# A fifth summed chunk in the up-projection's couples, and the convolution's two older taps multiplied on ScalarE

## The chip, the cores and the metric

One NeuronCore of a Trainium2 chip runs the whole program in one launch; the other cores do nothing. The metric is the device time of one execution in microseconds (us), the median of several. The engines are TensorE (PE in the profile, its weight loads PEld), VectorE (DVE), ScalarE (ACT), GpSimd (POOL) and SyncE (SP), which run side by side and wait for each other through semaphores.

## The reference

A trunk of two layers over 256 positions and 2048 features, in float32. Layer 0 mixes tokens with a gated MLP, layer 1 with latent attention. Behind each mixer comes the part that is changed here, an MLP with a causal convolution of width 3 along the positions:

```python
def conv_ffn(x, w_up, conv_w, conv_b, w_down):
    h = x @ w_up                                  # 2048 -> 2 * 5504
    h = depthwise_causal_conv(h, conv_w) + conv_b # h[s]*w2 + h[s-1]*w1 + h[s-2]*w0 + b, per column
    a, g = jnp.split(h, 2, axis=-1)
    return (jax.nn.silu(g) * a) @ w_down          # 5504 -> 2048
```

Each sub-layer ends in x = LayerNorm(ALPHA * x + sublayer(x)).

## The kernel before, in words

**Three products for one.** Each float32 operand is split into a high part that TensorE takes (`hi`) and the rest (`lo`); a product is hi*hi + lo*hi + hi*lo. Activations come split as `xhl`. Weights are streamed: `Feed` (line 86) loads chunks of 1 MB into tiles `raw` (3 slots), ScalarE casts the high part `wh` (line 134), VectorE subtracts for the low part `wl` (line 137), and both go into tiles with the tag `big` (14 slots in all, shared with `xhl` and much else). `next` (line 210) hands out one chunk and puts the split of the chunks two further on into the program. The tag `side` has 6 slots, `t1` (tiles of 256 columns) 6, `t2` (512 columns) 5. A planner orders each engine's instructions when the program is built; on the chip each engine then works through its own list in order.

**Wide and summed chunks.** A wide chunk covers two blocks of 128 of the contraction, two halves of 128 positions and two pieces of 512 columns: eight products of 512 columns, three matmuls each, 24 in all (`eight`, line 439). A summed chunk (kind `seven`, line 140) gets the same with seven products, 21 matmuls, by Strassen's scheme in Winograd's form. For that VectorE first forms four sums of its weights (`ts`: one instruction of 1024 columns and two of 512, lines 148 to 151), and these are split as well (`th`, `tl`, line 153): two casts and two subtractions of 1536 columns and one each of 512. The activations need sums too; `combine` (line 319) makes them once for each chunk position, in rooms that hold two positions each.

**The up-projection.** For each layer the 86 column blocks of 128 (43 of the half `a`, 43 of the half `g`) are worked off in groups of two blocks of each half (group 21 has one). Most groups are plain (`plain`, line 1081): weights stand still, positions stream, 4 chunks, 128 matmuls, half of them of 512 columns and half of 256, into 4 of the 8 PSUM banks. Groups 5 with 6 and 8 with 9 are done as couples (`summed`, line 1106) with 8 chunks of the two kinds into all 8 banks. The order of a couple's chunks is `UP_PAIRS` = 0, 2, 1, 3, 5, 4, 6, 7, and `UP_SEVEN` names the summed ones. Around the plain groups 1 to 4 the table `EARLY` (line 76) hangs the making of the activations' sums and other small jobs behind given chunks. A couple's outputs have the positions in rows; in the next plain group they are turned back by TensorE and then go through the convolution there (`both`, line 1051).

**The convolution.** `conv` (line 1018) works on one column block, 128 partitions of 256 positions. From a plain group it first adds the two halves of a bank (`sum_halves`, line 407: ScalarE copies one half to `lo`, VectorE adds the other into `h`), which is what frees the bank; from a couple it reads the bank itself. ScalarE writes the newest tap with its bias into `c` (line 1023), and VectorE adds the two older taps with one fused multiply-add each (lines 1024 and 1026). `pair` (line 1034) does this for a block of `a` and of `g`, then ScalarE takes silu (line 1040) and VectorE multiplies (line 1041).

Of the kernel before, what the change touches and what calls it, by code (L numbers as in the profile page):

```python
# [8 lines left out]
F32 = mybir.dt.float32  # L9
F32R = mybir.dt.float32r  # L10
BF16 = mybir.dt.bfloat16
AF = mybir.ActivationFunctionType
ALU = mybir.AluOpType
AX = mybir.AxisListType

P = 128
S = 256
# [36 lines left out]

MO_SEVEN = (1, 2)

T1, T2 = 6, 5
SLOTS = {"big": 14, "raw": 3, "side": 6}


# [11 lines left out]

UP = [(1,), (2,), (3,), (4,), (5, 6), (7,), (8, 9), *((i,) for i in range(10, 22))]
UP_PAIRS = [0, 2, 1, 3, 5, 4, 6, 7]
UP_SEVEN = (2, 3, 4, 6)
EARLY = {(1, 2): ("restore", 0), (2, 1): ("combine", 0), (2, 2): ("restore", 1), (2, 3): ("park", 0),
         (3, 1): ("restore", 2), (3, 2): ("combine", 1), (3, 3): ("restore", 3), (4, 0): ("park", 1),
         (4, 1): ("combine", 2), (4, 2): ("combine", 3)}


def plan(n_k):
# [140 lines left out]
def trunk(ctx: ExitStack, tc: tile.TileContext, x, xT, gm_in, gm_wout, ffn_up, ffn_dn,  # L222
          ml_q, ml_kv, ml_b, ml_out, consts, w_sT, b_s, ropes, ln_rows, out):
    nc = tc.nc
# [3 lines left out]
    tp = ctx.enter_context(tc.tile_pool(name="tp", bufs=3))  # L228
# [6 lines left out]
    def slot(shape, name, dt=F32, tag="big"):  # L235
        return big.tile(shape, dt, tag=tag, name=name, bufs=SLOTS[tag])

    def bank(name):
        return ps.tile([P, 512], F32, tag="bank", name=name)
# [21 lines left out]
    for g in range(6):  # L261
        for p in U_PAIRS[g]:
            i = 48 + 8 * g + p // 2
            w = gm_in[i : i + 5 : 4, :, p % 2 * 1024 : p % 2 * 1024 + 1024].rearrange("f p c -> p f c")
# [14 lines left out]
    def up(w):  # L279

        for gis in ((0,), *UP):
# [3 lines left out]
            for p in UP_PAIRS:  # L285
                i = 4 * gis[0] + p // 2
                t = w[i : i + 5 : 4, :, p % 2 * 1024 : p % 2 * 1024 + 1024].rearrange("f p c -> p f c")
                chunks.append((t, 2048, "seven" if p in UP_SEVEN else "wide"))

# [29 lines left out]
    def combine(name, o, k1, k2):  # L319


        t = tp.tile([P, 4, P], F32, tag="t2", name=f"xs{name}", bufs=T2)
        turn(t, k1, k2)
        o = o.rearrange("p (h s c) -> p h s c", h=2, s=4)
        nc.scalar.copy(o[:, 0], t)
        nc.vector.tensor_tensor(o[:, 1], t, o[:, 0].bitcast(F32), ALU.subtract)
        return [(o[:, 0, i], o[:, 1, i]) for i in (1, 2, 0, 3)]
# [29 lines left out]
    cst = cpool.tile([P, N_CONST], F32, name="cst")  # L357
# [49 lines left out]
    def sum_halves(acc, name):  # L407
        lo = tp.tile([P, S], F32, tag="t1", name=f"lo_{name}", bufs=T1)
        nc.scalar.copy(lo, acc[:, S : 2 * S])
        h = tp.tile([P, S], F32, tag="t1", name=f"h_{name}", bufs=T1)  # L410
        nc.vector.tensor_tensor(h, acc[:, 0:S], lo, ALU.add)
        return h

    def split_act(src, name):

# [443 lines left out]
    for gi in range(6):  # L859

        acc = Banks(f"v{gi}", DIRECT if gi == 0 else OWN + DIRECT if gi % 2 else DIRECT + OWN)
# [99 lines left out]
    def turned(g, tiles):  # L961

        for i, t in enumerate(tiles):
            src = v[g][:, i // 2, i % 2 * 512 : i % 2 * 512 + 512]
            for j in range(4):
                nc.tensor.transpose(t[:, j * P : (j + 1) * P], src[:, j * P : (j + 1) * P], ident)
            nc.scalar.copy(src, t)
# [15 lines left out]
    for g in range(6):  # L983
        direct, own = (ub[4:], ub[:4]) if g % 2 else (ub[:4], ub[4:])
        acc = Banks(f"u{g}", DIRECT + OWN, direct + own)
# [29 lines left out]
    acc, end = down(NF_GM, pT, "wo", ln, acts, tiles=ub, beside=lambda: turned(5, ub[4:]))  # L1015


    def conv(layer, F, acc, name):

        h = acc if acc.shape[-1] == S else sum_halves(acc, name)  # L1020
        w = C_CONV + (layer * 2 * NF_FF + F) * 4
        c = tp.tile([P, S], F32, tag="t1", name=f"c_{name}", bufs=T1)
        nc.scalar.activation(c, h, AF.Identity, bias=cst[:, w + 3 : w + 4], scale=cst[:, w + 2 : w + 3])
        nc.vector.scalar_tensor_tensor(c[:, 1:S], h[:, 0 : S - 1], cst[:, w + 1 : w + 2], c[:, 1:S],
                                       ALU.mult, ALU.add)
        nc.vector.scalar_tensor_tensor(c[:, 2:S], h[:, 0 : S - 2], cst[:, w : w + 1], c[:, 2:S],
                                       ALU.mult, ALU.add)
        return c

    def ffn(layer, ln, acc, end, last):  # L1030
# [3 lines left out]
        def pair(a, acc_a, acc_g):  # L1034
            if act[a // 8] is None:
                act[a // 8] = slot([P, 8, S], f"act{layer}_{a // 8}", tag="side" if a // 8 in (0, 5) else "big")
            ca = conv(layer, a, acc_a, f"{layer}a{a}")
            cg = conv(layer, NF_FF + a, acc_g, f"{layer}g{a}")
            s = tp.tile([P, S], F32, tag="t1", name=f"s{layer}_{a}", bufs=T1)
            nc.scalar.activation(s, cg, AF.Silu)  # L1040
            nc.vector.tensor_tensor(act[a // 8][:, a % 8, :], s, ca, ALU.mult)
# [26 lines left out]
        sums, rooms = {}, []  # L1068

        def combine_up(p):  # L1070

            x = xhl[p // 2][:, p % 2 * 2 : p % 2 * 2 + 2]
            y = tp.tile([P, 2, S], F32, tag="t2", name=f"upy{layer}_{p}", bufs=T2)
            nc.vector.tensor_tensor(y, x[:, :, 0:S].bitcast(F32), x[:, :, S : 2 * S].bitcast(F32), ALU.add)
            if len(sums) % 2 == 0:
                rooms.append(slot([P, 2, 8 * P], f"xu{layer}_{p}", F32R))
            sums[p] = combine(f"u{layer}_{p}", rooms[-1][:, len(sums) % 2, :], y[:, 0], y[:, 1])

        early = {"restore": old.restore, "park": old.park, "combine": lambda i: combine_up(UP_SEVEN[i])}

        def plain(gi, turned):
# [24 lines left out]
        def summed(gis):  # L1106

            acc = Banks(f"up{layer}_{gis[0]}", DIRECT + OWN)
            for p in UP_PAIRS:
                a = [[x_parts(xhl, 2 * p + j, b) for j in range(2)] for b in range(2)]  # L1110
                got = feed.next()
                if p in UP_SEVEN:
                    acc.seven(a, sums[p], *got, turned=512, across=True)
                    if p == UP_SEVEN[-1]:
                        rest = acc.rest()
# [16 lines left out]
    ln, acc, end = ffn(0, ln, acc, end, False)  # L1132
# [61 lines left out]
    acc = [[bank(f"mkv{b}_{f}") for f in range(2)] for b in range(2)]  # L1194
    for c in range(6):
        hi, lo = feed.next()
# [34 lines left out]
    acc = [[bank(f"qr{b}_{f}") for f in range(2)] for b in range(2)]  # L1231
    for c in range(2):
        hi, lo = feed.next()
# [145 lines left out]
    for hf in range(2):  # L1379
        acc = [[bank(f"vv{hf}_{b}_{f}") for f in range(2)] for b in range(2)]  # L1380
        for c in range(2):
            hi, lo = feed.next()
# [10 lines left out]
        for b in range(2):  # L1393
            for f in range(2):
                c = slice(hf * 1024 + f * 512, hf * 1024 + (f + 1) * 512)
# [14 lines left out]
    acc = [[bank(f"mo0_{b}_{f}") for f in range(2)] for b in range(2)]  # L1410
    LAG = 4
    attend_c(0)
    for t in range(3, H + LAG):
        k = t - LAG
        if k >= 0:
            if k % 2 == 0:
                hi, lo = feed.next()
            w = slice((k % 2) * 1024, (k % 2) * 1024 + 1024)
# [19 lines left out]
    for c in range(8):  # L1438
        left = 7 - c
        got = feed.next(splits=2 if left > 5 else 3, loads=2)  # L1440
        if left < SKEW:
            for j in range(2):
                w = slice(j * 1024, (j + 1) * 1024)
# [10 lines left out]
    acc = [[second.acc[DIRECT[2 * b + f]] for f in range(2)] for b in range(2)]  # L1454
# [6 lines left out]
    ln, acc, end = ffn(1, ln, banks, end_mo, True)  # L1461
# [99 lines left out]
```

## Time and profile before

| | |
|---|---|
| time, median of 3 runs | 2450.97 us (2450.84 to 2450.98) |
| profiled execution | 2450.69 us, its span 2448.9 us |
| granted TensorE clock | full in all 40 slices of the page |
| matmuls | 12154 |
| DMA | 627.37 MB, mean 256 GB/s |

The span is the time from the first to the last instruction of the profiled execution; its own time is measured around it. Busy time of an engine counts the stretches in which at least one of its instructions is under way. Instructions on one engine overlap by a little, so a sum of durations is somewhat more than the time that they take back to back.

### The profile page before, as it was taken

What the parts mean: (1) busy time and instruction counts of PE and PEld (TensorE: products, weight loads), DVE (VectorE), ACT (ScalarE), POOL (GpSimd) and SP (SyncE); (2) the same over time, 40 slices, a digit from 0 to 9 for tenths busy, and PEclk for the clock granted to TensorE, in tenths of its full rate; (3) what the DMA queues carried; (4) which work ended last, traced back from release to release, by engine and by line L of the source; (5) the groups of instructions that cost most, each with busy time, mean ns of one, the idle gap of its engine ahead of it and who ended that gap; (6) DMA issues with size and microseconds to landing.
All of it is one profiled execution on the core that took longest, in us unless ns stands there. A gap on an engine that the chain in (4) does not pass through costs nothing.

```text
span 2448.9 us, 32246 instructions
## 1 busy us (share of the span) xinstructions
PE 2441.2 (100%) x12154; PEld 2066.0 (84%) x12154; DVE 2187.1 (89%) x2909; ACT 1510.8 (62%) x1995; POOL 140.2 (6%) x261
## 2 busy tenths in 40 slices
PE   9999999999999999999999999999999999999999
PEld 7888888888888888888888888988888888888887
DVE  7999999889998889998889897878798998888998
ACT  6666665566576655666665566665665666666553
POOL 0000000001010000011000000000000001010000
PEclk9999999999999999999999999999999999999999
DMA  7555666658796655799988885543575589898894
GB/s 293 204 206 206 232 202 206 206 172 302 256 296 241 239 203 194 260 356 377 338 322 320 317 299 170 189 143 126 205 275 180 179 337 363 321 368 304 313 353 178
DMA packets 128763, 627.37 MB, mean 256 GB/s; under 512 B 11592, under 2 KB 15184, under 8 KB 91616
## 3 DMA queue, kind: packets, MB, share of 16 engines
q1 hardware_dynamic: 94224, 462.47, 53.1%
q0 software_dynamic: 34384, 162.86, 17.8%
q8 instruction: 95, 1.56, 0.2%
q14 instruction: 60, 0.49, 0.1%
HBM read 552.35 MB, written 72.93 MB: 255 GB/s over the span
## 4 chain that ended last, share of the span: by engine, by line
PE 95%; DVE 2%; issue 1%; DMA 1%; ACT 1%; SPq 0%; ACTq 0%; DVEq 0%
PE up L242 29%; PE ub L242 16%; PE dn_q L242 8%; PE dn_p L242 6%; PE v_q L242 5%; PE v_p L242 4%; PE up_q L242 2%; PE wo_q L242 2%; PE dn_e L242 2%; PE up_p L242 2%; PE wo_p L242 2%; PE upf L242 2%; PE mo L242 2%; PE v_e L242 2%; PE mkv L242 1%
## 5 line engine op out<-in xcount | busy, mean ns | idle before, releaser
L137 DVE TENSOR_TENSOR wl<-raw,wh 128x1024 fp32r<-128x1024 f32 (+5 forms) x611 | 937.7, 1553 | 106.3 <-ACT wh L134 76.3
L134 ACT CAST wh<-raw 128x1024 fp32r<-128x1024 f32 (+5 forms) x611 | 791.2, 1318 | 312.9 <-PE up L242 72.0
L242 PE MATMUL up<-xhl,wh 128*128 128x512 f32 x2112 | 492.9, 390 | 0.0
L242 PEld LDWEIGHTS up<-xhl,wh 128*128 128x128 f32 x2112 | 392.3, 188 | 78.6
L134 ACT CAST th<-ts 128x1536 fp32r<-128x1536 f32 x194 | 201.5, 1052 | 164.2 <-DVE ts L144 136.9
L242 PEld LDWEIGHTS up<-xhl,wl 128*128 128x128 f32 x2112 | 262.4, 192 | 5.1
L242 PE MATMUL up<-xhl,wl 128*128 128x256 f32 x2112 | 265.1, 283 | 0.0
L137 DVE TENSOR_TENSOR tl<-ts,th 128x1536 fp32r<-128x1536 f32 x194 | 229.6, 1223 | 9.1 <-ACT th L134 4.7
L242 PE MATMUL ub<-wh,xhl 128*128 128x512 f32 x564 | 175.7, 393 | 0.0
L144 DVE TENSOR_TENSOR ts<-ts,raw 128x512 f32<-128x512 f32 x194 | 133.9, 690 | 2.0
L242 PEld LDWEIGHTS ub<-wh,xhl 128*128 128x128 f32 x564 | 105.9, 188 | 23.7 <-issue 1.9
L144 DVE TENSOR_TENSOR ts<-raw 128x1024 f32<-128x1024 f32 x97 | 118.5, 1222 | 2.7 <-DMA raw<-in_gm_in_dram 1.0
L242 PE MATMUL ub<-wl,xhl 128*128 128x512 f32 x282 | 109.8, 389 | 0.0
L242 PE MATMUL v_q<-wh,xhl 128*128 128x512 f32 x224 | 70.7, 391 | 0.1
L242 PEld LDWEIGHTS ub<-wl,xhl 128*128 128x128 f32 x282 | 53.0, 188 | 11.1
L242 PE MATMUL v_p<-wh,xhl 128*128 128x512 f32 x192 | 59.9, 389 | 0.0
L242 PEld LDWEIGHTS v_q<-wh,xhl 128*128 128x128 f32 x224 | 42.1, 188 | 9.7 <-ACT wh L134 1.0
L832 ACT ACTIVATE lny<-lnt,lncol 128x128 f32<-128x128 f32 x96 | 36.5, 469 | 15.7 <-PE lnt L828 15.6
L161 DVE TENSOR_TENSOR praw<-praw 128x512 f32<-128x512 f32 x64 | 44.1, 690 | 0.5
L242 PE MATMUL v_q<-wl,xhl 128*128 128x512 f32 x112 | 43.6, 389 | 0.0
L242 PE MATMUL mo<-wh,oT 128*128 128x512 f32 x128 | 42.7, 411 | 0.0
L242 PEld LDWEIGHTS v_p<-wh,xhl 128*128 128x128 f32 x192 | 36.1, 188 | 7.5
(2073 smaller groups left out, 4820.9 us busy)
## 6 DMA issues: line engine op xcount, KB each, us to landing
raw<-in_ffn_up_dram SPq DMA_DIRECT2D x172, 1024.0 KB, 5.7
raw<-in_gm_in_dram SPq DMA_DIRECT2D x93, 1024.0 KB, 5.2
raw<-in_ffn_dn_dram SPq DMA_DIRECT2D x68, 1024.0 KB, 7.9
raw<-in_gm_wout_dram SPq DMA_DIRECT2D x48, 1024.0 KB, 6.5
praw<-in_ffn_dn_dram POOLq DMA_DIRECT2D x16, 1024.0 KB, 12.8
keptth<-pth POOLq DMA_DIRECT2D x16, 1024.0 KB, 8.5
kepttl<-ptl POOLq DMA_DIRECT2D x16, 1024.0 KB, 8.8
fth<-keptth POOLq DMA_DIRECT2D x16, 1024.0 KB, 9.6
```

What stands on the lines that cost most here:

```text
L134: cast = self.nc.scalar.copy(hi, raw)
L137: self.nc.vector.tensor_tensor(lo, raw, hi.bitcast(F32), ALU.subtract)
L144: add = lambda o, a, b: self.nc.vector.tensor_tensor(o, a, b, ALU.add)
L161: add = lambda o, a, b: pin(nc.vector.tensor_tensor(o, a, b, ALU.add))
L242: recent[0] = nc.tensor.matmul(o, l, r, start=start, stop=stop, skip_group_check=True)
L832: nc.scalar.activation(y[:, j], t[:, j * P : (j + 1) * P], AF.Identity, bias=lncol[:, o : o + 1], scale=lncol[:, g : g + 1])
```

## The change

Chunk position 5 of every couple is summed as well, so a couple's chunks are wide, summed, wide, four summed, wide. Its activations' sums are made behind the last chunk of group 4. The rooms of the activations' sums (three now, two before) lie in `side` instead of `big`. The two older taps of the convolution are multiplied by ScalarE into a tile `d`, which VectorE adds to `c`; the first `d` reuses the tile `lo` where there is one, the other is a new tile, and `t1` has 7 slots instead of 6.

```diff
-T1, T2 = 6, 5
+T1, T2 = 7, 5
 SLOTS = {"big": 14, "raw": 3, "side": 6}
...
-UP_SEVEN = (2, 3, 4, 6)
+UP_SEVEN = (2, 3, 5, 4, 6)
 EARLY = {(1, 2): ("restore", 0), (2, 1): ("combine", 0), (2, 2): ("restore", 1), (2, 3): ("park", 0),
          (3, 1): ("restore", 2), (3, 2): ("combine", 1), (3, 3): ("restore", 3), (4, 0): ("park", 1),
-         (4, 1): ("combine", 2), (4, 2): ("combine", 3)}
+         (4, 1): ("combine", 2), (4, 2): ("combine", 3), (4, 3): ("combine", 4)}
...
         nc.vector.tensor_tensor(h, acc[:, 0:S], lo, ALU.add)
-        return h
+        return h, lo
...
-        h = acc if acc.shape[-1] == S else sum_halves(acc, name)
+        h, spare = (acc, None) if acc.shape[-1] == S else sum_halves(acc, name)
         w = C_CONV + (layer * 2 * NF_FF + F) * 4
         c = tp.tile([P, S], F32, tag="t1", name=f"c_{name}", bufs=T1)
         nc.scalar.activation(c, h, AF.Identity, bias=cst[:, w + 3 : w + 4], scale=cst[:, w + 2 : w + 3])
-        nc.vector.scalar_tensor_tensor(c[:, 1:S], h[:, 0 : S - 1], cst[:, w + 1 : w + 2], c[:, 1:S],
-                                       ALU.mult, ALU.add)
-        nc.vector.scalar_tensor_tensor(c[:, 2:S], h[:, 0 : S - 2], cst[:, w : w + 1], c[:, 2:S],
-                                       ALU.mult, ALU.add)
+        for j in range(2):
+            d = spare if spare is not None and j == 0 else tp.tile([P, S], F32, tag="t1", name=f"d{j}_{name}", bufs=T1)
+            nc.scalar.mul(d[:, 1 + j : S], h[:, 0 : S - 1 - j], cst[:, w + 1 - j : w + 2 - j])
+            nc.vector.tensor_tensor(c[:, 1 + j : S], c[:, 1 + j : S], d[:, 1 + j : S], ALU.add)
         return c
...
             if len(sums) % 2 == 0:
-                rooms.append(slot([P, 2, 8 * P], f"xu{layer}_{p}", F32R))
+                rooms.append(slot([P, 2, 8 * P], f"xu{layer}_{p}", F32R, "side"))
```

## Rows read from the trace of the kernel before

**Rows 1.** The page, part 1: busy time, share of the span, instructions of each engine.
```profile
PE 2441.2 (100%) x12154; PEld 2066.0 (84%) x12154; DVE 2187.1 (89%) x2909; ACT 1510.8 (62%) x1995; POOL 140.2 (6%) x261
```

**Rows 2.** The chain that ended last: shares; and a piece (start, us, what).
```profile
PE 95%; DVE 2%; issue 1%; DMA 1%; ACT 1%; SPq 0%; ACTq 0%; DVEq 0%
...
1467.23 5.44 PE dn_q L242 x24
```

**Rows 3.** Waits of TensorE and its weight loads: us in total, times, longest.
```profile
PE up_p L242 <- DVE h_1a L411: 0.5, 1, 0.5
...
PEld up_q L242 <- DVE tl L137: 0.8, 2, 0.4
```

**Rows 4.** Stretch, length; busy us PE, PEld, DVE, ACT, POOL; clock; DMA share, GB/s.
```profile
812.17:900.20 88.03, 88.03 (x511) 78.08 (x511) 77.14 (x127) 50.16 (x73) 1.81 (x3) 1.00 0.74 255
900.20:941.00 40.80, 40.80 (x181) 33.80 (x180) 37.04 (x42) 25.10 (x27) 0.00 (x0) 1.00 0.52 184
941.00:964.97 23.97, 23.97 (x145) 21.42 (x144) 22.41 (x36) 14.38 (x21) 0.00 (x0) 1.00 0.56 195
964.97:1006.17 41.20, 41.20 (x181) 33.62 (x180) 38.85 (x44) 24.48 (x27) 0.00 (x0) 1.00 0.54 189
1006.17:1263.68 257.51, 257.51 (x1490) 228.31 (x1489) 229.57 (x324) 166.61 (x231) 24.33 (x43) 1.00 0.91 345
...
1919.90:1961.80 41.90, 41.39 (x181) 33.59 (x180) 38.99 (x45) 25.09 (x29) 0.00 (x0) 1.00 0.55 188
```

**Rows 5.** Groups by line on VectorE: shapes, count, busy us, mean ns, idle before.
```profile
L137 DVE TENSOR_TENSOR wl<-raw,wh 128x2048 fp32r<-128x2048 f32 x146 | 333.4, 2292 | 57.9 <-ACT wh L134 51.7 <-PE dn_q L242 3.8
L137 DVE TENSOR_TENSOR tl<-ts,th 128x1536 fp32r<-128x1536 f32 x97 | 170.4, 1757 | 9.1 <-ACT th L134 4.7 <-PE v_p L242 1.9 <-PE ub L242 1.4
L137 DVE TENSOR_TENSOR wl<-raw,wh 128x1536 fp32r<-128x1536 f32 x97 | 170.3, 1755 | 3.8 <-PE v_q L242 2.5 <-PE up L242 0.8 <-PE mo L242 0.3
L144 DVE TENSOR_TENSOR ts<-ts,raw 128x512 f32<-128x512 f32 x194 | 133.9, 690 | 2.0
L144 DVE TENSOR_TENSOR ts<-raw 128x1024 f32<-128x1024 f32 x97 | 118.5, 1222 | 2.7 <-DMA raw<-in_gm_in_dram 1.0 <-PE ub L242 0.7 <-PE v_q L242 0.5
L137 DVE TENSOR_TENSOR tl<-ts,th 128x512 fp32r<-128x512 f32 x97 | 66.8, 689 | 0.0
L1041 DVE TENSOR_TENSOR act<-s,c_1a 128x256 f32<-128x256 f32 x43 | 18.2, 424 | 5.1 <-ACT s L1040 5.0
L1024 DVE SCALAR_TENSOR_TENSOR c_0g<-h_0g,cst,c_0g 128x255 f32<-128x255 f32 x33 | 15.9, 481 | 3.0 <-ACT c_0g L1023 3.0
```

**Rows 6.** VectorE in order of time, layer 0's couples: start, us, line, operation, [idle before].
```profile
906.33 2.29 DVE L137 TENSOR_TENSOR wl<-raw,wh 128x2048 fp32r<-128x2048 f32 x1 [1.31 <-ACT wh L134]
...
908.94 0.42 DVE L411 TENSOR_TENSOR h_0g<-up,lo_0g 128x256 f32<-128x256 f32 x1
...
930.51 2.35 DVE L137 TENSOR_TENSOR tl<-ts,th 128x1536 fp32r<-128x1536 f32 x2
...
983.23 2.29 DVE L137 TENSOR_TENSOR wl<-raw,wh 128x2048 fp32r<-128x2048 f32 x1
985.44 1.22 DVE L144 TENSOR_TENSOR ts<-raw 128x1024 f32<-128x1024 f32 x1
...
991.84 1.22 DVE L144 TENSOR_TENSOR ts<-raw 128x1024 f32<-128x1024 f32 x1
```

**Rows 7.** TensorE in order of time, at the first couple's chunk 6.
```profile
933.30 0.39 PE L242 MATMUL up_q<-tl,xhl 128*128 128x512 f32 x1
```

**Rows 8.** Groups by line on ScalarE: the convolution's present operations.
```profile
L1023 ACT ACTIVATE c_0g<-h_0g,cst 128x256 f32<-128x256 f32 x10 | 6.0, 602 | 7.6 <-DVE h_0g L411 7.6
L1040 ACT ACTIVATE s<-c_0g 128x256 f32<-128x256 f32 x43 | 17.9, 416 | 22.1 <-DVE c_0g L1026 22.1
L409 ACT COPY lo_0a<-up 128x256 f32<-128x256 f32 x33 | 11.9, 361 | 23.0 <-PE up L242 23.0
```

**Rows 9.** TensorE's weight loads in order of time, the first couple's second chunk.
```profile
909.50 0.41 PEld L242 LDWEIGHTS up_p<-th,xu 128*128 128x128 f32 x2
```

## The prediction, made before the changed kernel was run

> **What bounds the kernel now.** I read the engines' totals first: TensorE is busy for 2441.2 of 2448.9 us, VectorE for 89%, ScalarE for 62% [rows 1]. A busy TensorE need not be one at its peak, so the second view is the chain of work that ended last: 95% of it is TensorE, and its pieces give the rate, 24 matmuls of 512 columns in 5.44 us, or 0.2267 us each [rows 2]. The third view, TensorE's waits, shows how little is lost beside that: the waits that touch this change are fractions of a microsecond, one for a sum of the convolution (h) and two for a low part (tl) of a summed chunk [rows 3]. So time can go in two ways only: by fewer matmuls, or by stalls that the other engines put between them.
>
> The stages that the change touches are read from busy times by stretch [rows 4]. In layer 0 they are: plain groups 1 to 4, the first couple (groups 5 and 6), plain group 7, the second couple (8 and 9), and plain groups 10 to 21. A couple of today needs four wide chunks of 24 matmuls and four summed ones of 21: 180 x 0.2267 = 40.80 us. The first couple takes exactly that. The second takes 41.20 in layer 0, and in layer 1 41.90. So today's stalls in the four couples are 0.40 + 1.10 = 1.50 us, all in the second ones. VectorE idles 10.9 us in the 88 before the first couple, 3.8 in it, and 3.9 in group 7 and the second couple together (65.17 less 22.41 and 38.85). That last stretch is where VectorE is nearly the bound as well.
>
> **The matmuls removed.** Chunk 5 of each couple turns from wide to summed: 24 products become 21. Two couples in each of two layers make 4 x 3 = 12 matmuls, 12 x 0.2267 = 2.72 us, all of it on the path. This is the whole direct gain, and 0.11% of the time.
>
> **What chunk 5 costs VectorE.** By mean durations [rows 5] a summed chunk is 1.222 + 2 x 0.690 + 1.755 + 1.757 + 0.689 = 6.80 us, a wide one 2.292. Back to back they overlap a little. In the second couple a wide chunk's subtraction starts at 983.23, the next summed chunk at 985.44 and the one behind it at 991.84, with VectorE never idle [rows 6]: 2.21 and 6.40 us. The change adds 4.19 us to each couple, while TensorE's need falls to 177 x 0.2267 = 40.12 us. The order in a couple becomes wide, summed, wide, four summed in a row, wide. In that run VectorE needs 6.40 us a chunk where TensorE needs 4.76, so it loses 1.6 us of its lead with each.
>
> That lead is thin today: the last low part of the first couple's chunk 6 is finished at 930.51 + 2.35 = 932.86, and TensorE starts on it at 933.30 [rows 6, 7].
>
> The fifth sum itself (combine 4, after group 4's last chunk) is one addition of 512 columns, four of 128 and one subtraction of 512 on VectorE, about 2 us, in a stretch with 10.9 us of idle time. I count it at nothing; without that cover it would be 2 us in each first couple.
>
> **What the convolution gives back.** A fused multiply-add takes 0.481 us, an addition of two tiles of 256 columns 0.424 [rows 5]: 0.057 saved for each tap. Both taps of the four convolutions of a plain group, or of the eight that a couple hands on, count; 172 convolutions have 344 taps, 19.6 us in all. But only what falls into the couples' stretches matters. The four convolutions of group 4 run in the first couple: 8 x 0.057 = 0.46 us. Group 7 and the second couple hold twelve (eight from the first couple, four of group 7): 24 x 0.057 = 1.37 us.
>
> By the Trainium skill (VectorE: DVE Perf Modes, Rules for kernel authors) chained operations gain nothing by fusing and the count of operations is what to lower; here the count stays the same, so by count the relief would be nothing. The rows show 0.057 for each tap, and I keep that. By the rule the sum below would be 2 x 1.37 = 2.7 us longer, 2453.4 us.
>
> **What the convolution costs ScalarE.** No row shows a multiplication of 256 columns by a per-partition factor. Below it are the plain copy from PSUM at 0.361 and an activation with neither such factor nor such bias at 0.416; above it is the one with both, at 0.602 [rows 8]. I take 0.51, the middle of the two nearest, and keep 0.36 and 0.60 as ends: 344 x 0.51 = 175 us (124 to 206), which takes ScalarE from 62% to about 69%. In groups 10 to 21 it is busy 166.61 of 257.51 us; some 52 convolutions add 53 us, 85%. TensorE waits for nothing in that stretch, and VectorE there gets lighter, so I cost this at nothing. Without that cover it is a rival below.
>
> **Slots.** The rooms for the sums move from the tag with 14 slots to the side tag: two slots more for split chunks from group 2 to the end of the second couple. Today the first couple's third chunk (wide, pair 1) could not be subtracted before 906.33, with VectorE idle 1.31 us before it [rows 6], while the couple began at 900.20: its second tile had to wait until the first chunk was through. With two slots more this subtraction (2.21 us) fits into the idle time ahead of the couple. The seventh small tile (T1) does not loosen the convolution: a pair of columns now takes nine tiles where it took seven.
>
> **The sum for VectorE.** First couple: 37.04 + 4.19 - 0.46 - 2.21 = 38.56 us of work in TensorE's 40.12. That leaves 1.56 us of idle time where 3.76 stand today, enough once the 1.31 is gone; I take no stall (0 to 4.0: if nothing moves ahead and all idle time stays, 40.77 + 3.76 - 40.12 = 4.4, less the lead of 0.4). Group 7 and second couple: 61.26 + 4.19 - 1.37 = 64.08 us of work in 23.97 + 40.12 = 64.09. VectorE would have to be busy without a gap, and it idles 3.91 us there now, waiting for ScalarE, which gets more to do. Ends: all idle time goes, no stall; all of it stays, 3.9 us. There is no room to run ahead here, so the new slots help less; I take half, 1.95 us for each.
>
> Sum against the profiled execution's 2450.69 us (its span of 2448.9 and 1.8 around it, which I leave as it is): -2.72 matmuls, -1.50 present stalls, + 2 x 1.95 new ones = -0.32, so 2450.37. The median of the runs lies 0.28 above that execution: 2450.65, in round figures 2450.6.
>
> **Rivals.** (A) VectorE closes up fully: the two slots and the lighter convolution remove every gap. For it: the gaps of rows 6 are waits for casts that stood behind a slot. Against: a stretch that needs 64.08 of 64.09. Time: -2.72 - 1.50 = -4.22, 2446.7. This is the floor, and it is still within 0.2% of today.
>
> (B) The other side: VectorE falls behind in all four couples. Place: the low parts of the four summed chunks in a row. Price: 4.0 us in each first couple and 3.9 in each second, 15.8 - 4.22 = +11.6, 2462.6. It comes out slower by over 0.2% once the stalls of the four couples sum to over 4.2 + 4.9 = 9.1 us. For it: leads of 0.4 us today. Against: the idle time ahead of the first couples.
>
> (C) The banks of the group before come free too late. A couple takes eight banks, so the four of group 4 must be read out within its first two chunks. Today the last sum h ends at 908.94 + 0.42 = 909.36, and TensorE loads the weights for that bank at 909.50 [rows 6, 9]. Now four multiplications of the pair before stand on ScalarE ahead of it, 4 x 0.51 = 2.0 us, and the copy of the next pair may wait for a small tile. For it: the wait for h in rows 3 is of this kind. Against: pair 1's split, which stood between those steps, moves ahead. Up to 2 us in each couple: +8, 2458.6.
>
> (D) ScalarE becomes a bound in groups 10 to 21: half a microsecond for each of 24 groups is +12, 2462.6. For it: 85% on an engine that works in order and waits for VectorE in between. Against: TensorE waits for nothing there now, and the low parts run chunks ahead. The Trainium skill (ScalarE: Activation LUTs, Rules for kernel authors) puts multiplications on VectorE, not ScalarE, and so speaks for this rival: the estimate from the rows agrees that the move costs more than it saves, 0.51 us on one engine for 0.057 on the other.
>
> (E) That the change does not do what it says: the slots stay unused since only three raw tiles exist and loads come late. Then first couples behave as in B and second ones as forecast: + 2 x 4.0 = 8, 2458.6.
>
> **Chances.** Forecast (stalls of 2 to 8 us in all) 0.55; A 0.20; B 0.08; C 0.07; D 0.05; E 0.05. About 0.2% (4.9 us) is what a measurement of this kernel can tell from no change. A and the forecast lie within it; faster than that needs time that the couples do not hold, 0.04. Slower takes B to E save their mild ends, and the forecast's upper tail: 0.18. Same: 0.78. The range runs from the floor, 2446.7, to 2458, just short of C and E in full.
>
> **What would show it.** Right: twelve matmuls fewer; first couples of about 40.1 us; TensorE waiting for tl or wl in the second couples for 1 to 3 us each; additions of 0.42 us in place of 0.48, multiplications near 0.5 on ScalarE; third chunk's subtraction before the couple begins. Wrong: waits of TensorE in plain groups (D), for h at a couple's start (C), or couples with no wait at all (A).

## The result, and the profile after

The change makes the kernel slower by a small, measurable amount: 2455.55 us (median of 18 runs, 2454.12 to 2457.91) for 2450.97 (18 runs, 2449.97 to 2452.34). The ratio is 1.0019, 95% interval [1.0012, 1.0026]: +4.6 us. I had forecast 2450.6, which is 0.4 below the kernel before; the time lies inside the forecast's range, but on the other side of the kernel before, and the fastest of its runs is slower than the slowest of the kernel before. The profiled execution took 2455.28 us, its span is 2453.5.

The first view is the page's row of totals, against [rows 1]. It has the twelve matmuls fewer and ScalarE's 67%.

```profile
PE 2440.6 (99%) x12142; PEld 2063.2 (84%) x12142; DVE 2190.2 (89%) x2941; ACT 1644.1 (67%) x2349; POOL 140.3 (6%) x261
```

The second view is the busy times by stretch, against [rows 4] (length; busy us of PE, PEld, DVE, ACT, POOL; clock; DMA share, GB/s). In order: plain groups 1 to 4, first couple, group 7, second couple, groups 10 to 21 of layer 0, then the two couples of layer 1.

```profile
812.17:900.48 88.31, 88.31 (x513) 78.31 (x512) 77.83 (x133) 62.35 (x106) 1.81 (x3) 1.00 0.73 261
900.48:943.58 43.10, 41.10 (x178) 32.87 (x177) 38.62 (x44) 28.79 (x36) 0.00 (x0) 1.00 0.41 141
943.58:967.55 23.97, 23.97 (x145) 21.41 (x144) 23.81 (x36) 19.58 (x35) 0.00 (x0) 1.00 0.69 242
967.55:1008.83 41.28, 40.44 (x179) 33.14 (x177) 40.17 (x49) 29.45 (x39) 0.00 (x0) 1.00 0.47 165
1008.83:1266.40 257.57, 257.57 (x1490) 228.29 (x1489) 226.34 (x326) 205.20 (x333) 24.38 (x43) 1.00 0.90 347
1857.71:1900.81 43.10, 41.09 (x178) 32.87 (x177) 38.62 (x44) 28.80 (x36) 0.00 (x0) 1.00 0.41 141
1924.79:1966.09 41.30, 40.46 (x179) 33.14 (x178) 40.03 (x49) 29.23 (x39) 0.00 (x0) 1.00 0.48 165
```

A couple now needs 40.12 us of matmuls. The first couples take 43.10, so each stands still for 2.98 us; the second ones stand still for 1.16 and 1.18. Against the kernel before, the first couples are 2 x 2.30 = 4.60 us longer, the second ones 0.08 longer and 0.60 shorter, and layer 0's couples start 0.28 us later, a shift that comes from ahead of 812 us: 4.36 of the 4.6 by which the span grew. The other stages have the length they had, to 0.3 us in sum.

The third view is what TensorE and its weight loads wait for, against [rows 3].

```profile
PE up_q L242 <- ACT th L134: 5.4, 6, 1.3
PE up_p L242 <- DVE h_0g L411: 0.2, 1, 0.2
PEld up_q L242 <- ACT th L134: 7.9, 6, 1.8
```

The 7.9 us of the weight loads are nearly the couples' whole 2 x 2.98 + 2.34 = 8.3. They name ScalarE's cast th. VectorE in order of time in the first couple (start, us, line, operation, [idle before]) shows why that name misleads:

```profile
905.69 0.42 DVE L1041 TENSOR_TENSOR act<-s,c_0a 128x256 f32<-128x256 f32 x1 [0.48 <-ACT s L1040]
906.03 0.42 DVE L411 TENSOR_TENSOR h_0a<-up,lo_0a 128x256 f32<-128x256 f32 x1
907.76 2.29 DVE L137 TENSOR_TENSOR wl<-raw,wh 128x2048 fp32r<-128x2048 f32 x1 [1.32 <-ACT wh L134]
...
918.25 1.22 DVE L144 TENSOR_TENSOR ts<-raw 128x1024 f32<-128x1024 f32 x1
...
924.65 1.22 DVE L144 TENSOR_TENSOR ts<-raw 128x1024 f32<-128x1024 f32 x1
925.90 0.69 DVE L144 TENSOR_TENSOR ts<-ts,raw 128x512 f32<-128x512 f32 x1
...
931.05 1.22 DVE L144 TENSOR_TENSOR ts<-raw 128x1024 f32<-128x1024 f32 x1
```

and ScalarE and the weight loads at the same place:

```profile
926.68 1.48 ACT L134 CAST th<-ts 128x1536 fp32r<-128x1536 f32 x1 [2.18 <-DVE ts L144]
```

```profile
928.21 0.19 PEld L242 LDWEIGHTS up_q<-th,xu 128*128 128x128 f32 x1 [0.93 <-ACT th L134]
```

From 907.76 on VectorE has no gap worth naming and makes a summed chunk every 6.40 us. TensorE has caught up with it; it waits for a cast that itself had waited 2.18 us for VectorE's sum ts. And the wide subtraction at 907.76 is the third chunk's, the one that I had put ahead of the couple: it starts 7.28 us after the couple's begin, where it started 6.13 us after it before [rows 4, 6], with the same idle time in front of it, 1.32 us. ScalarE's list says why:

```profile
900.00 0.37 ACT L409 COPY lo_0a<-up 128x256 f32<-128x256 f32 x1 [3.20 <-PE up L242]
...
905.24 0.42 ACT L1040 ACTIVATE s<-c_0g 128x256 f32<-128x256 f32 x1 [0.62 <-DVE c_0g L1027]
905.56 0.36 ACT L409 COPY lo_0a<-up 128x256 f32<-128x256 f32 x1
905.81 1.92 ACT L134 CAST wh<-raw 128x2048 fp32r<-128x2048 f32 x1
```

In the kernel before it stands in the same place:

```profile
904.13 0.35 ACT L409 COPY lo_0a<-up 128x256 f32<-128x256 f32 x1
904.38 1.92 ACT L134 CAST wh<-raw 128x2048 fp32r<-128x2048 f32 x1
```

The cast wh stands behind the whole convolution of group 4's first pair. Whatever slots are free, an engine that works through its list in order doesn't come to it before 905.81, though ScalarE had 3.20 us idle ahead of 900.00. So the question for the experiments was: the order of that list, the longer convolution, or the load of the fifth sum itself?

### The profile page after: what moved, and what is told of

It is laid out like the page before. It is cut to its first block, busy times and chain, and to the rows that moved or that the text cites. A ratio compares the mean times of both kernels' runs of the same rounds, so it can differ in the third digit from the quotient of the medians.

```text
span 2453.5 us, 32671 instructions
## 1 busy us (share of the span) xinstructions
PE 2440.6 (99%) x12142; PEld 2063.2 (84%) x12142; DVE 2190.2 (89%) x2941; ACT 1644.1 (67%) x2349; POOL 140.3 (6%) x261
## 3 DMA queue, kind: packets, MB, share of 16 engines
q8 instruction: 95, 1.56, 0.2%
## 4 chain that ended last, share of the span: by engine, by line
PE 93%; DVE 4%; ACT 1%; issue 1%; DMA 1%; POOL 0%; DVEq 0%; ACTq 0%; POOLq 0%
PE up L242 30%; PE ub L242 16%; PE dn_q L242 8%; PE dn_p L242 6%; PE v_q L242 5%; PE v_p L242 4%; PE wo_q L242 2%; PE dn_e L242 2%; PE wo_p L242 2%; PE upf L242 2%; PE mo L242 2%; PE v_e L242 2%; PE up_q L242 1%; DVE ts L144 1%; DVE wl L137 1%
## 5 line engine op out<-in xcount | busy, mean ns | idle before, releaser
L134 ACT CAST th<-ts 128x1536 fp32r<-128x1536 f32 x202 | 209.8, 1051 | 162.6 <-DVE ts L144 134.7
L137 DVE TENSOR_TENSOR tl<-ts,th 128x1536 fp32r<-128x1536 f32 x202 | 238.9, 1217 | 6.5 <-PE v_p L242 1.9
L832 ACT ACTIVATE lny<-lnt,lncol 128x128 f32<-128x128 f32 x96 | 36.7, 472 | 15.7 <-PE lnt L828 15.6
L173 DVE TENSOR_TENSOR ptl<-praw,pth 128x2048 fp32r<-128x2048 f32 x16 | 36.6, 2287 | 6.9 <-ACT pth L172 6.9
```

The source lines that it names most:

```text
L134: cast = self.nc.scalar.copy(hi, raw)
L137: self.nc.vector.tensor_tensor(lo, raw, hi.bitcast(F32), ALU.subtract)
L173: pin(nc.vector.tensor_tensor(lo[:, 0:cols], raw[:, o : o + cols], hi[:, 0:cols].bitcast(F32), ALU.subtract))
L832: nc.scalar.activation(y[:, j], t[:, j * P : (j + 1) * P], AF.Identity, bias=lncol[:, o : o + 1], scale=lncol[:, g : g + 1])
```

## The experiments

All times below are medians of 11 runs (of 5 for bigrooms), each beside runs of the kernel before on the same chip; the tables at the end of this section put them together. "After" is the changed kernel. The intervals reach some 2 us to either side, and TensorE's waits outside the up-projection differ between profiled executions too (for wl in dn_q 0.2 us in ahead4 and 1.6 in early_h4, stages that no run edits). So causes are read from the couples' stretches, and the times only agree with them or not.

**The order alone.** The split of the couple's third chunk, and with it the load of the chunk two further on, is put into the program ahead of group 4's convolution:

```diff
+            if gi in (4,):
+                feed.ahead(feed.used + 5, feed.used + 3)
             for f in range(nt // 2):
                 pair(2 * gi + f, acc[f], acc[nt // 2 + f])
```

> The changed kernel, and the split of the first couple's third chunk (wide, pair 1) is put into the program ahead of group 4's last convolutions instead of behind them. Order theory: the stall of the first couples (43.10 us each where 177 matmuls need 40.12) comes from that split's place on ScalarE's list, behind the convolution of the group before, so that VectorE idles 7.1 us between 897 and 908 us. Then the first couples fall to 40.2 to 41.0 us, VectorE is idle under 4 us in that stretch, the second couples stay at 41.3, and the time falls by 4 to 6 us against the changed kernel, to 2449.5 to 2451.5. ScalarE theory: it is the two multiplications more for each convolution that make the chain long, wherever the split stands; then the first couples stay above 42 us and the time above 2453.5.

Measured: 2449.51 us, ratio to before 0.9995 [0.9987, 1.0004]: 1.07 below the kernel before, where the changed kernel is 4.58 above it. The stretches of its four couples, in the columns of before:

```profile
900.53:941.22 40.69, 40.52 (x179) 33.07 (x177) 37.49 (x45) 27.13 (x35) 0.00 (x0) 1.00 0.47 160
965.18:1006.13 40.95, 40.63 (x178) 33.08 (x177) 39.60 (x47) 28.76 (x38) 0.00 (x0) 1.00 0.47 161
1854.67:1895.36 40.69, 40.52 (x178) 33.06 (x177) 37.49 (x45) 27.14 (x35) 0.00 (x0) 1.00 0.48 159
1919.33:1960.27 40.94, 40.63 (x179) 33.07 (x177) 39.58 (x47) 28.76 (x38) 0.00 (x0) 1.00 0.48 162
```

and its ScalarE and VectorE, ahead of the couple:

```profile
895.16 1.91 ACT L134 CAST wh<-raw 128x2048 fp32r<-128x2048 f32 x1 [1.04 <-PE up L242]
...
897.13 2.29 DVE L137 TENSOR_TENSOR wl<-raw,wh 128x2048 fp32r<-128x2048 f32 x1 [0.79 <-ACT wh L134]
```

The subtraction that was at 907.76 is done by 899.42, and 2.41 of the 2.98 us go in each first couple. The second couples, which I had expected to stay at 41.3, are 0.33 and 0.36 shorter as well. The four couples together are 5.5 us shorter than in the changed kernel, and that is nearly the whole difference of 5.65. Nothing else was edited, so this is the price of the order, given the fifth sum and the new convolution.

**The convolution, the fifth sum and the slots, each undone.** In the changed kernel: the fused convolution put back; four sums again; the rooms put back under `big`.

```diff
...
-            nc.scalar.mul(d[...], h[...], cst[...])                      # oldconv
-            nc.vector.tensor_tensor(c[...], c[...], d[...], ALU.add)
+        nc.vector.scalar_tensor_tensor(c[...], h[...], cst[...], c[...], ALU.mult, ALU.add)
...
-UP_SEVEN = (2, 3, 5, 4, 6)                                               # four
+UP_SEVEN = (2, 3, 4, 6)
...
-                rooms.append(slot([P, 2, 8 * P], f"xu{layer}_{p}", F32R, "side"))   # bigrooms
+                rooms.append(slot([P, 2, 8 * P], f"xu{layer}_{p}", F32R))
```

> The changed kernel with the convolution of before (fused multiply-add on VectorE); five summed chunks, the rooms in the side tag and seven small tiles stay. Order theory: the third chunk's split still stands behind group 4's first convolutions, which are some 1.3 us shorter on ScalarE; first couples 41.8 to 42.8 us, second couples 42 to 43.5 since VectorE's relief of 1.4 us is gone; time 2455 to 2458. ScalarE theory: without the multiplications the first couples come back to 40.2 to 41 us, time 2450 to 2452.5.

> The changed kernel with four summed chunks a couple, as before: new convolution, rooms in the side tag, seven small tiles. Order theory: VectorE has 4.2 us less to do in each couple, so no stall in the first couples (40.8 to 41.1 us) and less than before in the second (40.8 to 41.0); time 2449.3 to 2450.5, a little under the kernel before. ScalarE theory: the longer convolution chain stalls the first couples by itself, 41.5 to 43 us, time 2452 to 2455.

> The changed kernel with the rooms of the activations' sums back in the tag with 14 slots, three of them now. Order theory: the slots did not let the third chunk's split move ahead, so the first couples change little (42.5 to 44 us); in the second couples the slots are what let VectorE close its gaps (3.9 us idle before, 1.3 now), and with three slots fewer they grow from 41.3 to 43 to 44.5; time 2458 to 2463. If slots are no limit anywhere, the time stays within 1 us of the changed kernel.

Measured: oldconv 2453.31 us, 1.0011 [1.0002, 1.0020], first couples 42.20, second ones 41.41. I had expected 2455 to 2458, with 42 to 43.5 in the second couples: those need the new convolution less than I thought. With the fused convolution the cast of the third chunk comes 1.14 us earlier on ScalarE:

```profile
904.67 1.92 ACT L134 CAST wh<-raw 128x2048 fp32r<-128x2048 f32 x1
```

So the queue is shorter, but in the same order, and 2.08 us of each first couple stay lost: the longer convolution has 0.9 us of the 2.98, no more. `four` 2451.68 us, 1.0006 [0.9996, 1.0015]: I had expected less. Its couples need 40.80 us and take 41.26, 41.20, 41.26 and 41.22 where VectorE got lighter. TensorE's one wait that the profile names in the first couple, 0.2 of its 0.46 us (its weight loads wait 0.6 us for the same sum), is this:

```profile
PE up_p L242 <- DVE h_0g L411: 0.2, 1, 0.2
```

That is the wait for a bank of the group before, my rival C in small: the sum that frees the bank stands behind the first pair's multiplications. For the 0.4 us in the second couples the profile names no other engine. bigrooms 2466.28 us, 1.0064 [1.0051, 1.0076], above what I had expected: its first couples take 43.88 and 43.99 us and its second ones 46.05 and 46.00, so five sums without the slots in `side` would have cost 11 us more (15.7 above the kernel before, for 4.6).

**The slots alone, in the kernel before.** The edit is that of the change, `"side"` for the rooms, and nothing else.

> The kernel before with one edit: the rooms of the sums in the tag side, so two slots more for split chunks. My prediction's step on the slots said that the first couple's third chunk would then be subtracted before the couple; the order theory says that its cast keeps its place behind the convolution, so this subtraction starts within 0.5 us of 906.33 less any shift of the span, with 1 us or more of idle time before it, and first couples stay at 40.80. Second couples, where slots were short, gain: 40.8 to 41.1 for 41.20 and 41.90. Time 2449.3 to 2451.0 us.

Measured: 2449.32 us, 0.9994 [0.9985, 1.0003]. Its four couples:

```profile
900.12:940.92 40.80, 40.80 (x181) 33.78 (x180) 37.65 (x43) 25.54 (x28) 0.00 (x0) 1.00 0.50 176
964.89:1005.69 40.80, 40.80 (x182) 33.78 (x180) 38.65 (x48) 24.50 (x29) 0.00 (x0) 1.00 0.50 177
1854.84:1895.64 40.80, 40.80 (x181) 33.78 (x180) 37.66 (x43) 25.74 (x28) 0.00 (x0) 1.00 0.51 179
1919.61:1960.41 40.80, 40.80 (x182) 33.78 (x180) 38.65 (x48) 24.63 (x29) 0.00 (x0) 1.00 0.52 181
```

and VectorE in it, ahead of the couple and at the third chunk's subtraction:

```profile
900.05 0.42 DVE L411 TENSOR_TENSOR h_0a<-up,lo_0a 128x256 f32<-128x256 f32 x1 [4.61 <-ACT lo_0a L409]
...
906.25 2.29 DVE L137 TENSOR_TENSOR wl<-raw,wh 128x2048 fp32r<-128x2048 f32 x1 [1.31 <-ACT wh L134]
```

Two slots more take the second couples' stalls to nothing (41.20 and 41.90 before) and leave the first couple's third chunk where it was, with its 1.31 us of idle time [rows 6]. They do bring the second chunk's split forward: its last low part is done by 895.44 us, where it took until 899.51 before. VectorE then idles 4.61 us, enough for the third chunk's subtraction, which is not yet its turn. It is one edit of the change, and the span is 1.4 us shorter than that of the kernel before.

**The order in the kernel before, and with the fused convolution.** The same call as in ahead4, in groups 4 and 7, first in the kernel before, then in the changed kernel with the fused convolution.

> The kernel before, with nothing changed but the place of one split: the third chunk's split of each couple stands ahead of the last convolutions of group 4 and of group 7. Order theory: the place matters only where VectorE has no lead to spare; the first couples had no stall, so they stay at 40.80 us, the second ones fall from 41.2 and 41.9 to between 40.8 and 41.2; time within 1 us under the kernel before. If the place were worth its 5 us by itself, whatever the chunks, the time would be 2445 to 2446.

> Five summed chunks, the convolution of before, and the third chunk's split ahead of the last convolutions of groups 4 and 7. Order theory: first couples 40.1 to 40.5 us (42.20 with the old place), without the wait for h that is left in the run with the new convolution (40.69); second couples 41.2 to 42.2, bound by VectorE; time 2449 to 2451, so that the new convolution is worth under 1 us either way once the place is right. ScalarE theory: the old convolution is better by 2 us and more than the new one at the same place, 2447.5 or less.

Measured: before_ahead47 2451.86 us, 1.0003 [0.9994, 1.0012], longer than expected; oldconv_ahead47 2450.24, 0.9998 [0.9989, 1.0007]. In the first of them the early cast waits until 899.29 us for a low part on VectorE (for the slot that this gives back, as I read the releaser, which no run separates from another reason) and stands ahead of the copy that frees group 4's first bank. ScalarE:

```profile
899.29 1.91 ACT L134 CAST wh<-raw 128x2048 fp32r<-128x2048 f32 x1 [2.54 <-DVE tl L137]
901.11 0.36 ACT L409 COPY lo_0a<-up 128x256 f32<-128x256 f32 x1
```

Its first couples take 41.46 and 41.11 us for 40.80, and its second ones 41.17 and 41.88, so they did not fall as I had expected. Without the slots the early place does harm, and before_side showed that without the early place the slots leave the third chunk where it was. This run also shows that the cast at 904.38 in the kernel before was not held by a slot: here it starts 5 us earlier with the same slots. ahead4 has both, beside the change's other edits, and there the cast runs at 895.16: the early subtraction that I had put down to the slots came with the two together. (The kernel before with these two alone was not run.) With the fused convolution and five sums the first couples take 40.53, the second ones 41.08.

**What is left in the couples.** `order`: ahead4 with the wide chunk 7 ahead of the summed chunks 4 and 6, in all couples. early_h: ahead4, and in groups 4 and 7 all four sums h are made first and the fused convolution follows. early_h4: the same in group 4 alone. `both`: early_h4, and the order 0, 2, 1, 3, 5, 7, 4, 6 in the second couples alone. both_oldconv: `both` with the fused convolution everywhere.

```diff
-UP_PAIRS = [0, 2, 1, 3, 5, 4, 6, 7]                                      # order
+UP_PAIRS = [0, 2, 1, 3, 5, 7, 4, 6]
...
+            if gi in (4, 7):                                              # early_h
+                for f in range(2):
+                    ready[f] = [sum_halves(acc[f + 2 * n], ...)[0] for n in range(2)]
             for f in range(nt // 2):
-                pair(2 * gi + f, acc[f], acc[nt // 2 + f])
+                pair(2 * gi + f, acc[f], acc[nt // 2 + f], ready.get(f, (None, None)))
```

> The changed kernel with the split moved ahead in group 4, and the couples' chunks in the order 0, 2, 1, 3, 5, 7, 4, 6: the last wide chunk stands between the summed ones, so that VectorE gets back 3.2 us of lead there. If the run of four summed chunks is what is left of the stall in the second couples (40.95 us where 40.12 are needed), they come to 40.1 to 40.5 us, and the first ones lose 0.2 us of their 40.69. The sums behind the last chunk come later by a chunk, which may stall the next group's turning by up to 1 us. Time 2447.5 to 2450.

> The changed kernel with the split moved ahead in group 4; in groups 4 and 7 all four sums of bank halves (h) come first and the convolutions behind them are the fused ones of before. If the 0.6 us left in the first couples is the wait for the bank that h frees, they come to 40.1 to 40.3 us; VectorE has 0.5 us more to do in each couple, so the second ones stay at 40.9 to 41.4. Time 2448.3 to 2449.8.

> ahead4 with the four sums h of group 4 made first and the fused convolution there alone; group 7 stays as in the change. If the first couples' last 0.57 us are the wait for a bank of group 4 behind the new convolution's multiplications, they come to 40.1 to 40.3 us (40.18 with the same edit in groups 4 and 7), and the second couples stay at 40.9 to 41.0 as in ahead4; time 2448.2 to 2449.4 us. If the gain came from the lighter load on ScalarE in group 7 too, the first couples stay at 40.5 or more. The rest of the kernel is unchanged.

> early_h4 and, in the second couples alone, the wide chunk 7 ahead of the summed chunks 4 and 6. If two summed chunks in a row are what VectorE can bear and the lead does the rest, first couples 40.1 to 40.3 and second ones 40.4 to 40.7 us; of it 0.2 us may come back in the groups behind, as with the same order in both couples (257.75 for 257.35); time 2447.8 to 2449.2 us, below the kernel before by 1.8 to 3.2. If the order only moves the wait into the next group, the second couple and groups 10 to 21 together stay at 298.3 us and the time at that of early_h4.

> The fifth sum and the rooms in side with the early split, the early sums h of group 4 and the second order of chunks, and the fused convolution everywhere: what the convolution on ScalarE is worth once the order is mended. First couples 40.18 us as before (group 4 was fused already). In the second couples each fused tap costs VectorE 0.06 us more, 1.4 us with the group before, where it idles 2.6 us now: if that idle time takes it, they stay at 40.7 to 41.0 and the time at 2448.3 to 2449.8 us, so that the moved multiplications are worth nothing; if VectorE has no room, 41.3 to 41.9 and 2449.8 to 2451.2 us.

Measured: order 2450.07 us, 0.9997 [0.9988, 1.0006]; early_h 2449.67, 0.9993 [0.9984, 1.0002]; early_h4 2450.47, 0.9997 [0.9988, 1.0006]; both 2449.30, 0.9992 [0.9983, 1.0001]; both_oldconv 2448.22, 0.9989 [0.9980, 0.9998]. The last is the only one of these five whose interval excludes the time before. `order` came out 0.07 above what I had expected, and its second couples at 40.57 for 40.1 to 40.5. The couples of both_oldconv:

```profile
900.15:940.33 40.18, 40.18 (x179) 33.15 (x178) 38.78 (x46) 24.39 (x28) 0.00 (x0) 1.00 0.49 169
964.31:1004.68 40.37, 40.37 (x178) 33.15 (x177) 39.90 (x49) 24.93 (x32) 0.00 (x0) 1.00 0.46 156
1854.23:1894.41 40.18, 40.18 (x178) 33.15 (x177) 38.79 (x46) 24.54 (x28) 0.00 (x0) 1.00 0.49 170
1918.39:1958.72 40.33, 40.33 (x179) 33.14 (x177) 39.83 (x48) 24.87 (x31) 0.00 (x0) 1.00 0.46 157
```

With the sums h first and the fused convolution behind them, the first couples' remaining 0.57 us shrink to 0.06 (40.18). The edit does two things: with the fused convolution but without the sums first, in oldconv_ahead47, 0.41 us are left. So the rest of ahead4 goes with the two together; how much of it was the bank alone no run separates. early_h4 took 2450.47 us where I had expected at most 2449.4, and its second couples did not stay where I said: 41.79 and 41.25 for ahead4's 40.95. VectorE idles 1.80 us in its group 7 where it idled 0.57, and 1.07 of it is a weight load that lands late (`ts<-raw`, released by the DMA). So 1 us of VectorE's work slides from group 7 into the couple (busy 22.18 and 40.58 us for 23.39 and 39.60), and weight loads of the couple wait for banks of group 7, which they do not in ahead4:

```profile
PEld up_p L242 <- DVE h_0a L411: 0.6, 1, 0.6
PEld up_q L242 <- DVE h_0g L411: 0.4, 1, 0.4
```

I have not followed why the load is late, so this part stays open, and with it why the second couples of `both` (40.76 and 41.01) fell short of what I had expected. And both_oldconv did better than both of its cases: I had the fused taps down as a load on VectorE that its idle time might or might not take. VectorE is indeed busier, in layer 0's group 7 and second couple together by 62.94 - 62.12 = 0.82 us, but it idles 1.2 us less there (1.41 for 2.63), and TensorE's stalls in the second couples go from 0.64 and 0.89 us to 0.25 and 0.21. Each taken against its runs of the kernel before, the two times lie 1.1 us apart, as the stalls do, but that is less than their intervals. Where chunk 7 is taken earlier, some of the gain comes back behind the couples: groups 10 to 21 take 257.75 us in `order` and 257.66 in both_oldconv for 257.35.

The 2 x 2 of the change's parts, all with the rooms in `side` and the third chunk's cast in its old place (time less that of the kernel before beside it; stall of one first couple, one second couple, worked out from the stretches less 40.80 or 40.12). before_side has six small tiles `t1`, the other three have seven; no run tells what that alone does:

| | four sums | five sums |
|---|---|---|
| fused convolution | -1.75 us; 0, 0 (before_side) | +2.73; 2.08, 1.29 (oldconv) |
| multiplied on ScalarE | +1.10; 0.46, 0.41 (four) | +4.58; 2.98, 1.17 (after) |

By the medians the new convolution costs 2.9 us with four sums and 1.9 with five; the fifth sum costs 4.5 or 3.5, its twelve matmuls already taken off. By the stalls of the four couples, which carry less noise, the new convolution costs 1.74 us with four sums and 1.56 with five (8.30 for 6.74), and the fifth sum, less 2.72 for its matmuls, 4.0 or 3.8. With five sums the new convolution loses 0.9 us in each first couple and wins 0.1 in each second one. The slots take 1.5 us of stalls from the kernel before. And the other runs, the first seven with five sums, the rooms in `side` and the third chunk's cast moved:

| kernel | time less before | stall of one first and one second couple |
|---|---|---|
| ahead4 | -1.07 us | 0.57, 0.83 |
| oldconv_ahead47 | -0.75 | 0.41, 0.96 |
| early_h | -1.32 | 0.06, 1.10 |
| early_h4 | -0.60 | 0.06, 1.40 |
| order | -0.92 | 0.45, 0.45 |
| both | -1.77 | 0.06, 0.77 |
| both_oldconv | -2.89 | 0.06, 0.23 |
| before_ahead47 (four sums, cast moved) | +0.87 | 0.49, 0.73 |
| bigrooms (cast in its old place) | +15.70 | 3.8, 5.9 |

## Why the prediction was wrong, step by step

**The step that failed** is the one headed Slots: "With two slots more this subtraction (2.21 us) fits into the idle time ahead of the couple", and behind it the term "I take no stall (0 to 4.0: ..." for the first couples. I had read an idle time that ended with a cast as a cast that wanted a slot. It wanted its turn: on ScalarE's list it stands behind the first pair's convolution, in the kernel before (904.38) as in the changed one (905.81). before_side shows that slots alone don't move it, ahead4 that another place in the program does, given the slots. The term came out at 2 x 2.98 = 5.96 us, and with it alone the sum of -0.32 becomes +5.6; the second couples take back 1.6 of that. The upper end of that term, 4.0, was worked out for this very case ("if nothing moves ahead"), and rival E has its course, though not its cause: the slots were used, for the second couples.

**The second couples' stalls** were put at half of 3.9, 1.95 us each, and measured at 1.16 and 1.18. "So the new slots help less" was the wrong way round: the second couples are where the slots work, as bigrooms (46.05 us) and before_side (no stall at all) show. VectorE's idle time in layer 0's group 7 and second couple fell from 3.9 to 0.16 + 1.11 = 1.27 us. It did nearly close up, as rival A wanted, but in the couples of the other kind the order stood against it.

**The terms that held.** Twelve matmuls, 40.12 us for a couple: couples in which TensorE waits for nothing took 40.18 (both_oldconv). VectorE's rate in the run of four summed chunks: 6.40 us a chunk (918.25, 924.65, 931.05). The place of the stalls in the four chunks in a row, as rival B had it, at three quarters of its price and in two of the four couples. The two operations, from the groups by line of the changed kernel (shapes, count, busy us, mean ns, idle before):

```profile
L1026 ACT ACTIVATE lo_0g<-h_0g,cst 128x255 f32<-128x255 f32 x33 | 16.3, 495 | 0.0
L1027 DVE TENSOR_TENSOR c_0g<-c_0g,lo_0g 128x255 f32<-128x255 f32 x33 | 13.8, 418 | 7.8 <-ACT lo_0g L1026 7.8
```

The multiplication takes 0.495 us where I took 0.51, and the addition 0.418 in place of 0.481 [rows 5]. One multiplication starts 0.40 us after another (901.37 and 901.77 in the first couple), so ScalarE's busy time grows by 133 us in all, not by the 175 that I summed from durations. But the last column has what I left out. Ahead of these 33 additions, the first ones of block g in layer 0, VectorE idles 7.8 us, waiting for the multiplication, where it idled 3.0 ahead of the 33 fused ones [rows 5]. Over both blocks and both layers that waiting grows from 7.0 + 3.0 + 7.0 + 3.0 = 20.0 us to 6.2 + 7.8 + 6.0 + 8.1 = 28.1, about what these 132 taps save at 0.06 each. I priced the operations and not the hop between the engines. Where it matters, in group 4's first pair, VectorE waits for a multiplication in the changed kernel:

```profile
901.90 0.42 DVE L1027 TENSOR_TENSOR c_0a<-c_0a,lo_0a 128x255 f32<-128x255 f32 x1 [1.07 <-ACT lo_0a L1026]
...
904.25 0.42 DVE L1027 TENSOR_TENSOR c_0g<-c_0g,lo_0g 128x255 f32<-128x255 f32 x1 [1.07 <-ACT lo_0g L1026]
```

and in oldconv for the newest tap:

```profile
901.51 0.48 DVE L1024 SCALAR_TENSOR_TENSOR c_0a<-h_0a,cst,c_0a 128x255 f32<-128x255 f32 x1 [0.67 <-ACT c_0a L1023]
...
903.00 0.48 DVE L1024 SCALAR_TENSOR_TENSOR c_0g<-h_0g,cst,c_0g 128x255 f32<-128x255 f32 x1 [0.28 <-ACT c_0g L1023]
```

These are 1.19 us more, and the third chunk's cast comes 1.14 us later.

By the Trainium skill (ScalarE: Activation LUTs, Rules for kernel authors) a multiplication belongs on VectorE; the reason that it gives is the rate for an element, with a figure for bf16. The stalls in the four couples come out on that side: 1.74 us in `four` and none in before_side, 1.65 in `both` and 0.58 in both_oldconv. Here the data is float32, and as far as the rows show the reason is the wait and the place in the list, not that rate.

**The rivals.** D is out: groups 10 to 21 keep their length with ScalarE busy for 205.20 of 257.57 us, 80%. C is there in small, at most 0.46 us of each first couple in `four`. A's 2446.7 was not reached: with the order mended, and without the new convolution, both_oldconv took 2448.22.

## What to carry to other kernels

An idle time that ends with a cast may want a slot or its turn in the list: look at what the casting engine does just before it, and if it is busy with, or waiting for, something unrelated that stands ahead, more slots won't move it. Where instructions are placed by their position in the program, move the call, and see that the slot is free by then; here either alone did nothing for the first couples, or harm. An operation split over two engines is priced with its hop: take the idle time ahead of the second half from the rows, not its duration alone, and look for the hop in the stretch that has no time to spare.

## What the runs showed of the hardware that I had not expected

ScalarE's price of one operation on some 256 columns rises with its per-partition operands: 0.416 us with neither [rows 8], 0.495 with a factor, 0.60 with factor and bias. The three are also different functions (silu, a multiplication, the newest tap), and no run changes the operands alone. 254 or 255 columns make no difference that the rows show (494 to 496 ns).
